# Expert weights in 8 KB rows from mixed buffers, and the second expert's slots mirrored

## The chip, the cores and the metric

The kernel runs on one core of a Trainium2 chip. The metric is the device time in microseconds (us) of one execution. The kernel before took 617.83 us, the median of three runs (617.82 to 617.93).

## The reference

One layer of a streaming encoder on 512 tokens of 1024 channels, in float32: a mixer (pooling and sparse attention), cross-attention to 256 memory tokens, and a mixture of experts (MoE). The change touches how the MoE gets its weights and its rows. Cut to that:

```python
g_sel  = argmax(hf @ wg_router + bg_router)              # one of 4 groups per token
e_in   = (hf @ we_router + be_router)[group g_sel]       # 8 experts of that group
top_v, top_i = top_k(e_in, 2)                            # two experts per token
top_w  = softmax(top_v) * softmax(group logits)[g_sel]
for each expert e of 32:                                 # w_gate, w_up: 1024 x 256; w_down: 256 x 1024
    out += (silu(hf @ w_gate[e]) * (hf @ w_up[e]) * gate[:, e]) @ w_down[e]
```

The weights of the 32 experts are 96 matrices of 1 MB. With these inputs an expert is chosen by 16 to 53 tokens.

## The kernel before

**Tiles and stages.** Tokens lie in 4 blocks of 128 (t = 0 to 3). The mixer and the cross-attention take the first 350 us or so; large products there are made of three products of split operands (`mm3`, L346 to L348). For each block, `wo_proj(t)` then adds the attention output to the residual tile `x[t]`, and `ffn_in(t)` turns `x[t]` by PE transposes (L1115) into `xT`, copied out by ACT (L1117, first half) and DVE (L1123), sums its squares on ACT (L1118), writes `x[t]` to the two DRAM tensors `hd` and `out` on ACT's DMA queue (L1119, L1121), and makes the router's logits on PE (L1129), which DVE scales (L1133) and ranks.

**The MoE.** Experts are taken in 16 pairs. A pair has 128 rows, one per partition: the first expert's tokens in partitions 0 to 63 (`CAP` = 64), the second's in 64 to 127. `select` (L1030) compares each token's place within its expert with a row of numbers 1 to 64 (`iota`), and `tables` makes from that, by matmuls, the token number of each row; empty rows get a number out of range, and are left out by the DMA. `fetch` gathers the rows of a pair from `hd` into one of two `g` buffers, `turn_rows` transposes them, `gate_up` and `down` are the matmuls (L1037), with the SiLU on ACT (L1227), and the result is added into `out` by an indirect DMA on POOL's queue (L1253, one row of 4 KB per token). The `g` buffers are zeroed once by ACT (L1019), in `buffer`, which the program calls after `ffn_in(3)`; the scheduler puts the instructions ahead of that block's copy on ACT.

**Buffers and loads.** Weights, split operands and other tiles live in slots of 4 KB per partition: 42, and 8 more once the attention's own pool is closed. A free list gives the slot that has been free longest. `Stream` keeps the list of loads in order and issues the next one, on SP's queue (L251), whenever enough slots are free (`pump`, called at each `put`). An expert matrix is two loads of 512 KB, one for each half of its rows (c = 0, 1), of 4 KB per partition: 192 loads in the order gate, up, down of a pair, half by half and expert by expert. SP's DMAs and ACT's share 8 completion lanes; a DMA waits for the one before it on its lane.

**The mark.** When the gates are known, SP issues a DMA of four bytes, `mark` (L1290), which stands in program order ahead of all loads that the program issues later: no load listed behind it starts earlier. 38 half matrices are listed ahead of it. Behind it comes the last write to `out` (L1291), then the loads. Ahead of both, in SP's queue, stands the read of `nover` (L1309), the number of extra passes, which is 0 with these inputs.

## Time and profile before

| | us |
|---|---|
| median of three runs | 617.83 |
| the profiled execution | 616.63 |
| its span, first to last instruction | 614.4 |
| PE busy | 554.3 (90%) |
| DVE, ACT, POOL busy | 303.7, 193.9, 114.0 |
| mean granted TensorE clock | 0.98 |

The profile is one execution. PE is the matmul engine, PEld its weight load, DVE, ACT and POOL the vector, scalar and GpSimd engines, SP the queue that issues the loads. In a list in order of time a row is start (us), duration (us), engine, line, operation, output<-input with sizes, and in brackets the idle time of the engine ahead of it and what ended it. A name with a q (SPq, ACTq) is an instruction of the engine's queue, such as the issue of a DMA. In a table by stretch a row has the stretch, its length, then busy time and number of instructions of each engine, the granted clock, the mean busy share of the 16 DMA engines and what they moved in GB/s. Queue q1 holds SP's loads, q10 ACT's writes, q0 the indirect DMAs; a row of a queue has packets, MB and the time of its packets as a share of 16 engines. A share above 1 comes from packets that overlap on an engine.

### The profile page before, as it was taken

To read this page: it belongs to the slowest core of one execution; us is meant where nothing else is said; L and a number is where in the kernel's file an instruction comes from. 1 tells how busy PE (TensorE), PEld (TensorE's weight loads), DVE (VectorE), ACT (ScalarE), POOL (GpSimd) and SP (SyncE) were. 2 spreads that over 40 slices of the span, in tenths; PEclk is the share of its full clock that TensorE was granted. 3 is DMA by queue.
4 is the path that set the end of the run, shared out by engine and by line. 5 is a ranking of instruction groups with operands and counts; after the bars stand their busy time and mean duration, and the time that the engine had idled before them with its cause. 6 is when DMAs were issued, how large, how long until landed. Compare 5 with 4: busy or idle time off the path is not lost. (4 is left out here: it accounts for less than half of the span.)

```text
span 614.4 us, 9117 instructions
## 1 busy us (share of the span) xinstructions
PE 554.3 (90%) x3414; PEld 384.8 (63%) x3414; DVE 303.7 (49%) x767; ACT 193.9 (32%) x368; POOL 114.0 (19%) x92
## 2 busy tenths in 40 slices
PE   8998989999999999999989879999999997778871
PEld 4786766888777777788868755555555543344430
DVE  3398999999976756544434632122223211111200
ACT  4374534434456557764432200000010000000000
POOL 0334330201372000030000111111112210111111
PEclk8998998999999999999999999999999999999896
DMA  8963022226661201128999699999999999999961
GB/s 286 387 214 103 2 69 86 87 66 226 209 237 36 79 1 35 67 73 254 351 328 375 232 375 408 396 379 385 368 381 359 344 356 369 371 361 361 367 219 28
DMA packets 52836, 147.87 MB, mean 241 GB/s; under 512 B 10290, under 2 KB 11058, under 8 KB 52786
## 3 DMA queue, kind: packets, MB, share of 16 engines
q1 hardware_dynamic: 47170, 135.15, 60.1%
q0 software_dynamic: 4608, 8.40, 5.6%
q10 hardware_dynamic: 1008, 3.67, 1.5%
q8 instruction: 29, 0.48, 0.3%
q14 instruction: 21, 0.17, 0.1%
HBM read 142.99 MB, written 12.58 MB: 253 GB/s over the span
## 5 line engine op out<-in xcount | busy, mean ns | idle before, releaser
L1037 PE MATMUL mm<-s,s 128*64 128x256 f32 x1024 | 124.6, 385 | 22.7 <-DMA s<-in_w_up_dram 9.8
L346 PE MATMUL mm<-s,s 128*128 128x512 f32 (+1 forms) x320 | 131.8, 415 | 1.1 <-ACT s L261 0.9
L347 PE MATMUL mm<-s,s 128*128 128x512 f32 (+1 forms) x320 | 127.6, 399 | 0.3 <-DVE s L268 0.3
L348 PE MATMUL mm<-s,s 128*128 128x512 f32 (+1 forms) x320 | 127.6, 399 | 0.0
L1037 PEld LDWEIGHTS mm<-s,s 128*64 128x64 f32 x1024 | 75.1, 137 | 68.3 <-ACT sg L1227 16.7
L1228 DVE SCALAR_TENSOR_TENSOR sg<-mm,gc,sg 128x256 f32<-128x256 f32 x16 | 7.7, 484 | 131.6 <-PE mm L1037 131.6
L346 PEld LDWEIGHTS mm<-s,s 128*128 128x128 f32 (+1 forms) x320 | 60.3, 189 | 18.2 <-issue 3.4
L1037 PE MATMUL mm<-s,hT 128*64 128x512 f32 x256 | 68.2, 604 | 3.4 <-DVE hT L1237 1.6
L348 PEld LDWEIGHTS mm<-s,s 128*128 128x128 f32 (+1 forms) x320 | 60.7, 190 | 13.8 <-issue 0.9
L347 PEld LDWEIGHTS mm<-s,s 128*128 128x128 f32 (+1 forms) x320 | 60.7, 190 | 13.5 <-issue 1.2
L1253 POOL DMA_INDIRECT out_dram<-s,idx x16 | 25.3, 1584 | 194.7 <-DVE s L1086 160.7
L263 POOL TENSOR_TENSOR s<-s,s 128x1024 fp32r<-128x1024 f32 x17 | 41.8, 2467 | 73.5 <-ACT s L261 73.5
L261 ACT CAST s<-s 128x1024 fp32r<-128x1024 f32 (+1 forms) x42 | 42.5, 1021 | 34.5 <-DMA s<-in_xattn_wkv_dram 8.1
L1250 ACT COPY s<-mm 128x512 f32<-128x512 f32 x16 | 9.4, 586 | 130.3 <-PE mm L1037 130.3
L1037 PEld LDWEIGHTS mm<-s,hT 128*64 128x64 f32 x256 | 20.1, 138 | 42.0 <-issue 24.3
L1251 DVE COPY s<-mm 128x512 f32<-128x512 f32 x16 | 11.1, 692 | 59.4 <-PE mm L1037 59.4
L1227 ACT ACTIVATE sg<-mm,gc 128x256 f32<-128x256 f32 x16 | 7.6, 473 | 101.3 <-PE mm L1037 101.3
L263 DVE TENSOR_TENSOR s<-s,s 128x1024 fp32r<-128x1024 f32 (+1 forms) x25 | 28.9, 1159 | 6.2 <-ACT s L261 4.8
L591 DVE MAX8 m<-s 128x8 f32<-128x256 f32 (+2 forms) x48 | 26.6, 553 | 0.3
L592 DVE MATCH_REPLACE8 s<-m,s 128x256 f32<-128x256 f32 (+2 forms) x48 | 26.0, 541 | 0.0
L687 ACT ACTIVATE p<-p,rsm,fq 128x128 f32<-128x128 f32 (+3 forms) x32 | 20.6, 646 | 6.6 <-DVE rsm L685 6.5
L356 PE MATMUL sc<-s,s 64*128 64x256 f32 (+3 forms) x216 | 22.0, 323 | 0.0
(212 smaller groups left out, 682.0 us busy)
## 6 DMA issues: line engine op xcount, KB each, us to landing
s<-in_w_up_dram SPq DMA_DIRECT2D x64, 512.0 KB
s<-in_w_gate_dram SPq DMA_DIRECT2D x64, 512.0 KB
s<-in_w_down_dram SPq DMA_DIRECT2D x64, 512.0 KB
s<-in_w_in_dram SPq DMA_DIRECT2D x20, 512.0 KB
s<-in_x_dram SPq DMA_DIRECT2D x8, 512.0 KB
s<-in_xattn_wkv_dram SPq DMA_DIRECT2D x8, 512.0 KB
s<-in_w_out_dram SPq DMA_DIRECT2D x8, 512.0 KB
s<-in_xattn_wq_dram SPq DMA_DIRECT2D x4, 512.0 KB
```

The costliest lines, as they stand in the source:

```text
L261: act.copy(hi, raw)
L263: eng.tensor_tensor(lo[:, c], raw[:, c], f32(hi[:, c]), op=OP.subtract)
L346: pe.matmul(ps, ah, bh, start=start, stop=False)
L347: pe.matmul(ps, ah, bl, start=False, stop=False)
L348: pe.matmul(ps, al, bh, start=False, stop=stop)
L356: pe.matmul(ps[i], a(i, qa), b(i, qb), start=(n == 0), stop=(n == 2), skip_group_check=True)
L591: dve.max(m8, a)
L592: dve.match_replace(a, m8, a, TAKEN)
L687: act.activation(ph, ph, AF.Exp, bias=m[:, h, 1:2], scale=f[:, h:h + 1], accum_out=m[:, h, 2:3])
L1037: return tc.keep_in_program_order(pe.matmul(*a, **k))
L1251: dve.tensor_copy(y[:, 512:], py[1])
L1253: pool.indirect_dma_start(out=out, out_offset=bass.IndirectOffsetOnAxis(ap=tabs_.pop(i)["idx"], axis=0), in_=y, in_offset=None, bounds_che ...
```

## The change

Three things change. First, the buffers: 18 slots of 4 KB and 12 of 8 KB (4 more of 8 KB later) stand in place of 42 (and 8) of 4 KB. The capacity is the same. A pair of split operands takes one 8 KB slot, and `N_OWN` slots of 4 KB are held back for the MoE's own tiles. Second, an expert matrix is one entry of the stream. It is loaded whole, by one DMA of 1 MB in rows of 8 KB per partition, into an 8 KB slot; where two 4 KB slots have been free for longer, it is loaded as two halves into these. In the MoE that makes 117 loads, 75 of 1 MB and 42 of 512 KB, in place of 192. Third, the second expert of a pair is mirrored: its first token has partition 127, its second 126, and so on, through a second row of numbers 64 to 1 beside `iota` (`seat`). Besides, the read of `nover` is written ahead of the first pass.

```diff
-NSLOT = 42
-NSLOT2 = 8
+N_ONE, N_TWO, N_TWO_MORE, N_OWN = 18, 12, 4, 7
...
+    def get_pair(self, shape, dt):
+
+        if not self.free2:
+            return [self.get(shape, dt) for _ in range(2)]
+        s = self.free2.pop(0)
+        t = self.tile(s, [P, 2, *shape[1:]], dt)
+        self.left[s] = 2
+        return [self.hold(t[:, i], s, t) for i in range(2)]
+
+    def get_whole(self, shape):
+
+        two, ones = self.free2[:1], self.free1[:2] if len(self.free1) >= 2 + self.owed else []
+        when = lambda v: max(self.freed[s] for s in v)
+        half = [shape[0], shape[1] // 2, *shape[2:]]
+        if two and (len(ones) < 2 or when(two) <= when(ones)):
+            s = self.free2.pop(0)
+            t = self.tile(s, shape, F32)
+            self.left[s] = 2
+            h = shape[1] // 2
+            return [(slice(None), t)], [self.hold(t[:, i * h:(i + 1) * h], s, t) for i in range(2)]
+        h = shape[1] // 2
+        parts = [self.get(half, F32) for _ in range(2)]
+        return [(slice(i * h, (i + 1) * h), p) for i, p in enumerate(parts)], parts
+
+    def room(self, shape, keep):
+        if int(np.prod(shape[1:])) <= 1024:
+            return len(self.free) >= 1 + keep
+        return len(self.free) >= 2 + keep and (bool(self.free2) or len(self.free1) >= 2 + self.owed)
 
     def take_out(self):
-        return self.free.pop(0)
+        self.owed = max(0, self.owed - 1)
+        return self.free1.pop(0)
...
     def do_load(src, shape):
+        if int(np.prod(shape[1:])) > 1024:
+            loads, parts = S.get_whole(shape)
+            for c, t in loads:
+                ins = sp.dma_start(t, src[:, c])
+                if held_back:
+                    tc.keep_in_program_order(ins)
+            return parts
...
-        hi, lo = S.get(shape, F32R), S.get(shape, F32R)
+        hi, lo = S.get_pair(shape, F32R)
...
+    seat = keep.tile([P, 2, CAP], F32, name="seat")
+    act.copy(seat[:, 0], iota)
+    dve.tensor_scalar(seat[:, 1], iota, -1.0, float(CAP + 1), op0=OP.mult, op1=OP.add)
...
-        s4 = sels[j].rearrange("p t (e c) -> p t e c", c=CAP)
+        s4 = sels[j].rearrange("p t (i e c) -> p t i e c", e=2, c=CAP)
         for t in tiles:
-            dve.tensor_tensor(s4[:, t], posp[:, t, 4 * j:4 * j + 4, None].to_broadcast([P, 4, CAP]),
-                              iota[:, None, :].to_broadcast([P, 4, CAP]), op=OP.is_equal)
+            dve.tensor_tensor(s4[:, t], posp[:, t, 4 * j:4 * j + 4].rearrange("p (i e) -> p i e", e=2)[:, :, :, None]
+                              .to_broadcast([P, 2, 2, CAP]), seat[:, None].to_broadcast([P, 2, 2, CAP]), op=OP.is_equal)
...
-            for c in range(2) if 0 <= i < NPR else ():
-                for k, e in enumerate(pairs[i]):
-                    w = A[f"w_{name}"][e]
-                    if name == "down":
-                        src, shape = w.rearrange("(p k) d -> p k d", k=2)[:, c], [P, D]
-                    else:
-                        src, shape = w.rearrange("(p k) f -> p k f", k=NC)[:, 4 * c:4 * c + 4], [P, 4, FF]
-                    ST.add((n, i, name, k, c), src, shape, eng="raw")
+            for k, e in enumerate(pairs[i] if 0 <= i < NPR else ()):
+                m = {"down": 2, "gate": NC, "up": NC}[name]
+                ST.add((n, i, name, k), A[f"w_{name}"][e].rearrange("(p k) f -> p k f", k=m), [P, m, 2048 // m], eng="raw")
...
     ST.pump()
+    n_extra = nc.values_load(nover, min_val=0, max_val=T // CAP - 1)
     moe_pass(0)
-    n_extra = nc.values_load(nover, min_val=0, max_val=T // CAP - 1)
```

The orders of the instructions move in three places. First ACT at the last block of tokens, before: `x[2]`'s write to `out`, the zeroing of the two `g` buffers, the copy of `xT` for block 3, its sum of squares and the write to `hd`.

```order
L1121 DMA out_dram<-s_150_1569 128x1024 [waits DMAHW3_49]
L1019 ACTIVATE s_272_3360<-cst 128x1024 [waits PE_49]
L1019 ACTIVATE s_273_3362<-cst 128x1024 [waits PE_49]
L1117 COPY s_270_3302<-tr 128x512 [waits PE_49]
L1118 ACTIVATE s_271_3303,s_2922<-s_151_1583 128x1024 [waits DVE_49]
L1119 DMA hd<-s_151_1583 128x1024 [waits DMAHW7_49]
L1196 ACTIVATE s_274_3385<-s_274_3385 128x4x4 [waits DVE_49]
```

And now, with the same places at L1207, L1105, L1203, L1204, L1205:

```order
L1207 DMA out_dram<-s_111_1530 128x1024 [waits DMAHW4_49]
L1105 ACTIVATE s_199_3275<-cst 128x1024 [waits DMAHW2_49,DMAHW4_49,PE_49,Activation_49]
L1203 COPY s_197_3217<-tr 128x512 [waits PE_49]
L1204 ACTIVATE s_198_3218,s_2867<-s_112_1544 128x1024 [waits DVE_49]
L1205 DMA hd<-s_112_1544 128x1024 [waits DMAHW7_49]
L1105 ACTIVATE s_200_3277<-cst 128x1024 [waits DVE_49,PE_49,Activation_49]
L1283 ACTIVATE s_201_3300<-s_201_3300 128x4x4 [waits DVE_49]
```

The first zeroing now has a slot that held `x[2]`, and waits for lanes 2 and 4, those of `x[2]`'s writes to `hd` and `out`; the copy stands behind it. The second zeroing stands behind the write of block 3.

Then SP from the mark on, before:

```order
L1309 TENSOR_LOAD nover [waits DVE_49]
L1309 ISA x2
L1290 DMA mark<-s_274_3385 1x1 [waits DMAHW0_49,DVE_49]
L1291 DMA out_dram<-s_151_1583 128x1024 [waits DMAHW1_49]
L251 DMA s_275_3418<-in_w_up_dram 128x1024 [waits DMAHW2_49]
L251 DMA s_276_3420<-in_w_up_dram 128x1024 [waits DMAHW3_49,PE_49,Activation_49]
L251 DMA s_277_3422<-in_w_down_dram 128x1024 [waits DMAHW4_49,Activation_49]
L251 DMA s_278_3424<-in_w_down_dram 128x1024 [waits DMAHW7_49,DMAHW5_49,DMAHW1_49]
L251 DMA s_279_3426<-in_w_down_dram 128x1024 [waits DMAHW6_49,PE_49]
L251 DMA s_282_3497<-in_w_down_dram 128x1024 [waits PE_49]
L251 DMA s_283_3499<-in_w_gate_dram 128x1024 [waits DMAHW0_49,PE_49]
```

And now:

```order
L1377 DMA mark<-s_201_3300 1x1 [waits DMAHW1_49,DVE_49]
L1378 DMA out_dram<-s_112_1544 128x1024 [waits DMAHW2_49]
L328 DMA s_202_3333<-in_w_up_dram 128x2048 [waits DMAHW3_49,PE_49]
L328 DMA s_203_3335<-in_w_down_dram 128x1024 [waits DMAHW4_49,Activation_49]
L328 DMA s_204_3336<-in_w_down_dram 128x1024 [waits DMAHW5_49,DMAHW7_49,DMAHW2_49,PE_49]
L1395 TENSOR_LOAD nover [waits DVE_49]
L1395 ISA x2
L328 DMA s_207_3422<-in_w_down_dram 128x2048 [waits DMAHW6_49,PE_49]
L328 DMA s_208_3424<-in_w_gate_dram 128x1024
L328 DMA s_209_3425<-in_w_gate_dram 128x1024 [waits DMAHW0_49]
```

Behind the mark there are now one whole matrix and two halves (4 halves in all) ahead of a whole `down` matrix that waits for PE; the read of `nover` stands behind the mark and not ahead of it.

And SP at the end of the first pass, before (`down` of the last pair, half by half):

```order
L251 DMA s_456_4824<-in_w_down_dram 128x1024 [waits DMAHW0_49,PE_49]
L251 DMA s_457_4826<-in_w_down_dram 128x1024 [waits DMAHW1_49,PE_49]
L251 DMA s_458_4828<-in_w_down_dram 128x1024 [waits DMAHW2_49,PE_49]
L251 DMA s_460_4844<-in_w_down_dram 128x1024 [waits DMAHW3_49,PE_49]
L1310 COMPARE_AND_BRANCH
```

And now, by whole matrices:

```order
L328 DMA s_323_4615<-in_w_up_dram 128x2048 [waits DMAHW5_49,PE_49]
L328 DMA s_324_4635<-in_w_up_dram 128x2048 [waits DMAHW6_49,PE_49]
L328 DMA s_325_4637<-in_w_down_dram 128x2048 [waits DMAHW7_49,PE_49]
L328 DMA s_327_4653<-in_w_down_dram 128x2048 [waits DMAHW0_49,PE_49]
L1397 COMPARE_AND_BRANCH
```

The last DMA of the pass is the second expert's whole `down` matrix; before it was the second half of it.

## Rows read from the trace of the kernel before

**Rows 1.** busy tenths in 40 slices of the span, from the page

```profile
PE   8998989999999999999989879999999997778871
...
DMA  8963022226661201128999699999999999999961
```

**Rows 2.** by stretch: busy of PE, PEld, DVE, ACT, POOL, clock, DMA share, GB/s

```profile
375.00:400.00 25.00, 23.31 (x174) 13.18 (x172) 7.03 (x18) 2.12 (x4) 5.31 (x4) 1.00 1.03 398
```

**Rows 3.** ACT, L1227, start, us; one per pair

```profile
451.51 0.47 ACT L1227 ACTIVATE sg<-mm,gc 128x256 f32<-128x256 f32 x1 [5.33 <-PE mm L1037]
...
465.47 0.47 ACT L1227 ACTIVATE sg<-mm,gc 128x256 f32<-128x256 f32 x1 [6.49 <-PE mm L1037]
...
563.74 0.47 ACT L1227 ACTIVATE sg<-mm,gc 128x256 f32<-128x256 f32 x1 [5.41 <-PE mm L1037]
...
588.33 0.47 ACT L1227 ACTIVATE sg<-mm,gc 128x256 f32<-128x256 f32 x1 [5.99 <-PE mm L1037]
```

**Rows 4.** as 2, from the router to the first pair

```profile
344.00:347.00 3.00, 2.21 (x26) 2.12 (x25) 2.76 (x20) 0.52 (x2) 0.00 (x0) 1.00 0.40 161
347.00:350.00 3.00, 2.16 (x20) 2.00 (x19) 2.01 (x14) 0.00 (x0) 0.54 (x1) 1.00 0.08 29
```

**Rows 5.** SP queue, start, us, from 337 us

```profile
337.66 1.06 SPq L251 DMA_DIRECT2D s<-in_w_up_dram  x2
349.60 0.73 SPq L1290 DMA_DIRECT2D mark<-s  x1
...
350.79 1.21 SPq L251 DMA_DIRECT2D s<-in_w_up_dram  x2
352.10 6.43 SPq L251 DMA_DIRECT2D s<-in_w_down_dram  x4
358.63 2.11 SPq L251 DMA_DIRECT2D s<-in_w_gate_dram  x3
```

**Rows 6.** ACT in order of time, the last token block

```profile
332.76 0.36 ACTq L1121 DMA_DIRECT2D out_dram<-s  x1
...
338.40 1.05 ACT L1019 ACTIVATE s<-cst 128x1024 f32<-128x1024 f32 x1 [1.46 <-PE mm L348]
339.36 0.57 ACT L1117 COPY s<-tr 128x512 f32<-128x512 f32 x1
339.83 1.06 ACT L1118 ACTIVATE s<-s 128x1024 bf16<-128x1024 f32 x1
```

**Rows 7.** DMA packets by queue, 334 to 342 us

```profile
q1 hardware_dynamic: 585, 2.14, 69.2%
q10 hardware_dynamic: 288, 1.05, 32.1%
```

**Rows 8.** PE, the last router projection, L1129

```profile
339.98 1.98 PE L1129 MATMUL mm<-s,s 128*128 128x36 f32 x16
```

**Rows 9.** DVE behind it

```profile
343.38 0.26 DVE L1133 SCALAR_TENSOR_TENSOR s<-mm,s,rgb 128x36 f32<-128x36 f32 x1 [0.66 <-POOL s L244]
```

**Rows 10.** PE, first pair, gate matmuls

```profile
356.24 3.67 PE L1037 MATMUL mm<-s,s 128*64 128x256 f32 x32 [0.33 <-DVE s L1086]
```

**Rows 11.** as 2, full queues: rows of 2 KB, then of 4 KB

```profile
20.00:28.00 8.00, 8.00 (x36) 6.14 (x35) 1.72 (x5) 1.49 (x2) 4.78 (x2) 1.00 1.04 398
585.80:590.00 4.20, 3.08 (x25) 1.95 (x27) 0.00 (x0) 0.47 (x1) 1.55 (x1) 1.00 1.03 415
```

**Rows 12.** as 2, around the last weights

```profile
590.00:592.00 2.00, 1.83 (x16) 1.05 (x14) 0.00 (x0) 0.00 (x0) 0.00 (x0) 1.00 1.01 318
...
594.00:598.60 4.60, 4.08 (x12) 1.06 (x12) 0.42 (x1) 0.00 (x0) 0.00 (x0) 1.00 0.06 20
```

**Rows 13.** as 2, in the last scatter

```profile
607.00:607.50 0.50, 0.00 (x0) 0.00 (x0) 0.00 (x0) 0.00 (x0) 0.00 (x0) 0.50 0.38 74
```

**Rows 14.** PE, a down projection in mid-stage

```profile
375.21 3.60 PE L1037 MATMUL mm<-s,hT 128*64 128x512 f32 x16
```

**Rows 15.** PE, the last one

```profile
598.87 1.93 PE L1037 MATMUL mm<-s,hT 128*64 128x512 f32 x6 [0.15 <-SPq L1310]
```

More of the change, by code (lines that the diff above doesn't have):

```diff
@@ L61, with __init__ @@
 class Slots:
-    def __init__(self, pool, n):
-        self.pools, self.free, self.n, self.where = {}, [], 0, {}
-        self.on_put = lambda: None
-        self.more(pool, n)
-    def more(self, pool, n):
-        self.pools.update({s: pool for s in range(len(self.pools), len(self.pools) + n)})
-        self.free += list(self.pools)[-n:]
-    def get(self, shape, dt):
-        s = self.free.pop(0)
-        self.n += 1
-        t = self.pools[s].tile(shape, dt, tag=f"s{s}", name=f"s{s}_{self.n}")
-        self.where[id(t)] = (s, t)
-        return t
+    def __init__(self, pool, ones, twos):
+        self.pool_of, self.free1, self.free2, self.spare = {}, [], [], []
+        self.where, self.left, self.n, self.clock = {}, {}, 0, 0
+        self.freed = {}
+        self.owed = N_OWN
+        self.on_put = lambda: None
+        self.more(pool, ones, twos)
@@ new lines, in more, with free, tile @@
+    def more(self, pool, ones, twos):
+        for k, (free, n) in enumerate(((self.free1, ones), (self.free2, twos))):
+            for _ in range(n):
+                s = len(self.pool_of)
+                self.pool_of[s] = pool
+                self.freed[s] = 0
+                free.append(s)
+    @property
+    def free(self):
+        return range(len(self.free1) + 2 * len(self.free2) + len(self.spare))
+    def tile(self, s, shape, dt):
+        self.n += 1
+        return self.pool_of[s].tile(shape, dt, tag=f"s{s}", name=f"s{s}_{self.n}")
@@ new lines, in hold @@
+    def hold(self, v, s, of):
+        self.where[id(v)] = (s, of, v)
+        return v
+    def get(self, shape, dt):
+        if self.free1:
+            s = self.free1.pop(0)
+            return self.hold(self.tile(s, shape, dt), s, None)
+        n = int(np.prod(shape[1:]))
+        names = "abc"[:len(shape) - 1]
+        at = next((p for p in self.spare if p[2] == dt), None)
+        if at is None:
+            s = self.free2.pop(0)
+            t = self.tile(s, [P, 2, 1024], dt)
+            self.left[s] = 1
+            half = 0
+            self.spare.append((s, t, dt))
+        else:
+            self.spare.remove(at)
+            s, t, _ = at
+            self.left[s] += 1
+            half = 1
+        v = t[:, half, :n]
+        if len(names) > 1:
+            v = v.rearrange(f"p ({' '.join(names)}) -> p {' '.join(names)}", **dict(zip(names, shape[1:])))
+        return self.hold(v, s, t)
@@ L87, in put @@
+    again = tile
     def put(self, *tiles):
+        self.clock += 1
         for t in tiles:
-            self.free.append(self.where.pop(id(t))[0])
+            s, of, _ = self.where.pop(id(t))
+            if of is None:
+                self.free1.append(s)
+            else:
+                self.left[s] -= 1
+                if self.left[s]:
+                    continue
+                self.spare = [p for p in self.spare if p[0] != s]
+                self.free2.append(s)
+            self.freed[s] = self.clock
@@ L130, in pump @@
                 self.out_next()
-            elif (self.n_load < len(self.items) and len(self.S.free) >= 1 + keep
+            elif (self.n_load < len(self.items) and self.S.room(self.items[self.n_load][2], keep)
                   and (len(self.raw) < self.raw_max)):
@@ L503, in evac_k @@
         if t % 2 == 0:
-            kT[t // 2] = [S.get([P, 2, 4, P], F32R) for _ in range(2)]
+            kT[t // 2] = S.get_pair([P, 2, 4, P], F32R)
         WV.defer(PRM['lat'], lambda: split_T(qr, kT[t // 2][0][:, t % 2], kT[t // 2][1][:, t % 2], ("kT", t)))
@@ L601, in load_bands @@
     def load_bands():
-        pw["b"] = [S.get([P, 1024], F32R) for _ in range(2)]
+        pw["b"] = S.get_pair([P, 1024], F32R)
         pw["w"] = S.get([P, 4, P], F32)
@@ L752, in memory @@
         dve.tensor_tensor(gqk, vecs[:, V_QN:V_QN + 1], vecs[:, V_KN:V_KN + 1], op=OP.mult)
-        kmT.extend(S.get([P, MH, MT], F32R) for _ in range(2))
+        kmT.extend(S.get_pair([P, MH, MT], F32R))
         vm.append(S.get([P, 2, 512], F32))
@@ L831, in transposed @@
     def transposed(t):
-        hl = [S.get([P, NC, P], F32R) for _ in range(2)]
+        hl = S.get_pair([P, NC, P], F32R)
         for k in range(2):
@@ L1217, in gate_up @@
         for u, name in enumerate(("gate", "up")):
-            W = {(k, c): ST.take((n, i, name, k, c)) for c in range(2) for k in range(2)}
+            W, held = expert(n, i, name)
             for c in range(NC):
@@ L1240, in down @@
     def down(n, i, hT):
-        W = {(k, c): ST.take((n, i, "down", k, c)) for c in range(2) for k in range(2)}
+        W, held = expert(n, i, "down")
         y = own("y", i % 2, [P, D], F32)
```

20 lines of the change are left out of this document (11 added, 9 removed).

## The prediction

> **What bounds the kernel now.** I read the slices of the span first, then the table by stretch, then the places where a saturated engine stops. The slices [rows 1] show two regimes: PE full and the DMA engines mostly idle for the first half, then both full from slice 24 on, the MoE. From 375 us the DMA share is 1.03 at 398 GB/s [rows 2]. Which of the two sets the pace there is read from the SiLU of each pair [rows 3]: 13.96 us from 451.51 to 465.47, where PE eats weights fetched ahead, but 24.6 us from 563.74 to 588.33, near the end, where PE waits for weights. So the end of the kernel is the end of the DMA stream that starts behind the mark, plus a tail. In front of it lies a hole: the DMA share is 0.40 in 344 to 347 us and 0.08 in 347 to 350 [rows 4], because SP issues a load at 337.66, then nothing until the mark at 349.60 [rows 5]. A us lost by the mark, or a us in which the queues run dry behind it, is a us at the end. At the far end one engine works alone: 318 GB/s in 590 to 592 us, then 20 GB/s at a share of 0.06, one of sixteen, until the last matmuls start at 598.87 [rows 12, 15].
>
> **The change part by part.** All times are against the profiled execution (616.63 us; span 614.4 and 2.2 us around it). The median shown is 1.20 us above it, and I add that at the end.
>
> *The zeroing on ACT.* This is the part that I think costs most. Before, the second zeroing starts at 338.40 and the copy of block 3 follows at 339.36 [rows 6]; neither waits for a DMA. Now the first zeroing waits for the writes of `x[2]`, and the copy stands behind it. The write to `out` is issued at 332.76 [rows 6]. Between 334 and 342 us ACT's queue moved 288 packets of 1.05 MB in all [rows 7], which is exactly the two writes of 512 KB, so they are through by about 342.0. The zeroing then runs to 343.06 (1.06), the copy to 343.63 (0.57), and the router's matmuls, 1.98 us [rows 8], to 345.6. The other branch, the sum of squares behind the copy (1.06 us) and the power on POOL, ends at about the same time. DVE's scaling of the logits started at 343.38 [rows 9] and would start at 345.7: the gates, the mark and the first gather are 2.3 us later, with the queues already dry. Bounds: 1.0, if the writes land 1.3 us sooner; 4.8, if they land 2.5 us later because each write packet of 4 KB now takes turns with load packets of 8 KB (the queue is then through as late as 344.5, where the share drops in [rows 4]). Value +2.3.
>
> *Loads behind the mark.* Before, nine halves follow the mark between 350.79 and 360.7 (2, 4 and 3 in [rows 5]), each as soon as one slot is free. Now four halves can go, and the fifth entry, a whole `down` matrix, needs both halves of an 8 KB slot, which the first gate matmuls hold: these run from 356.24 for 3.67 us [rows 10], so it is issued at 359.9, and nothing behind it can overtake it. The four halves, the last write and two gathers are 2.1 + 0.5 + 0.45 MB, about 3.05 MB (the gathers are 112 rows of 4 KB by the routing), 7.5 us at 410 GB/s, between [rows 2] and [rows 11], from about 352.5: dry from 360 to the first bytes of the new load. Those come 2 us after its issue by my estimate; the write issued at 332.76 [rows 6] had all its packets behind 334 [rows 7], so it is more than 1.2. That is 2 us. Bounds 0.5 (the writes and gathers stretch over it) and 4.0 (a second such hole about 372 us, where the next whole loads wait for the second pair). Value +2.0.
>
> *The tail.* The last DMA now brings the whole `down` matrix of the second expert, and each of its packets holds both halves of a row, so only 2 of the 16 matmul instructions of `down` can run before it lands, where 10 could. Sixteen take 3.60 us in mid-stage [rows 14], 0.225 each; the last six took 1.93 [rows 15]. Eight more behind the last byte: +1.8, and at least 1.2 if the last packets' landing is spread.
>
> *Rows of 8 KB.* Nothing in the trace has them. Full queues moved 398 GB/s with rows of 2 KB and 415 with 4 KB [rows 11]: 2.513 and 2.410 us per MB, 0.103 less for a doubling. If it is a fixed cost per row, the next doubling saves half as much, 0.052 us per MB. Behind the mark 60 whole loads bring 62.9 MB: 3.2 us. Bounds: 0 (the rows are cut to 4 KB on the way) and 5 (the whole 0.103 carries over, less what two queues already overlap). Value -3.0. Twice the bytes in flight on the same lanes bring nothing, since the share is 1.03 already [rows 2].
>
> *The mirror.* Does it level the engines? The gather and the scatter give each engine the rows of fixed partitions, and the routing of these inputs (worked out from the reference) fills the low places of each half. In the last scatter, 53 and 34 rows, the share is still 0.38 at 607.0 to 607.5 [rows 13], about five or six of sixteen. If the 16 engines each took four neighbours of 64 partitions, and both experts so, eight engines would have a second helping; if eight engines serve the first half and eight the second, five have it. The row speaks for the second. Then engine sums over all pairs are 86 rows at most in the first half and 101 in the second, and mirroring turns the second eight around: the heaviest is still 101. Value 0; the price if it does level them is the second rival's. The extra row of numbers is one instruction each on ACT and DVE at the very start, where PE does not yet work at its full share [rows 1] and loads set the pace, and the read of `nover` moves off SP's path to the mark, but the gates that the mark waits for come after it on DVE anyway: 0, and half a us either way for the early loads, which I take as covered by PE's full slices [rows 1].
>
> Sum: 2.3 + 2.0 + 1.8 - 3.0 = +3.1 on 616.63, 619.7; with 1.20 for the median, **620.9 us**. All lows together give -2.3, all highs +10.6; they are unlikely together, so the likeliest case's own range is 618.9 to 624.5.
>
> **The rivals.**
>
> *The mirror levels the engines (0.12).* For it: one engine ends seven or eight us behind the others (they stop within 590 to 592, PE's last weights come just before 598.87 [rows 12, 15]), so there is a load to level. Against it: [rows 13]. If the heavy places of the two experts do share engines, the lone stretch goes, up to 8 us, and 620.9 falls to about 613.
>
> *Rows of 8 KB pay and the holes don't show (0.20).* If the writes land early and the 8 KB saving is at its bound, the sum of lows holds: 615.5. For it: the loads are most of the bytes. Against it: both waits stand in the order of the instructions.
>
> *The parts cancel (0.18).* With 8 KB at -4 and the two holes at their lower halves, the sum is between -1.2 and +1.2: 616.6 to 619.
>
> *The mirrored heavy engine is slow (0.05).* The last places of the second half now fill first, so the engine of partitions 92 to 95 and 124 to 127 carries 101 rows and sets the end over 246 us. If it were 1% slower than the one that sets it now, the end would move by 2.5 us: 623.4. It decides as soon as that engine is slower at all, since no other has as much to do. Nothing in the rows shows a slow engine: with all of them full the sum is 415 GB/s [rows 11] and the lone one at the end moves 20 [rows 12], of which its share is near a sixteenth of that. The Trainium skill, on the page "DMA: Bandwidth & Descriptors", section "Latency and other measured facts", says that engines 7 and 15 are usually slower than the rest where POOL issues DMAs; by that rule the result would be on this side, and the trace so far does not bear it out.
>
> *8 KB rows are cut to 4 KB (inside the forecast's 0.45).* Then the third term is 0 and the time 623.9.
>
> **How the numbers follow.** The forecast with its upper end has 0.45, the slow engine 0.05: slower 0.50. Same, 0.18. Faster, 0.32 (0.20 and 0.12). Two tenths of a per cent, 1.2 us, is about what this kernel's measurement can tell. The range reaches down to the second rival, 613, and up to 625, a little above the cut rows with a late write; about 2 in 10 lie outside.
>
> **What would show it.** In the changed profile the first zeroing (L1105) should start about 342 with a DMA as its releaser, and the mark near 352; if the mark is at 349.6, the first term is wrong. SP should issue one `down` load when the first gate matmuls end, with a DMA share under 0.8 in the 3 us around it. The q1 packets should be 8 KB, and full stretches should show 420 to 425 GB/s; 415 would mean no saving. A single engine should still end alone for about 8 us; if all engines end together, the mirror works and I am wrong by its price. Behind the last load 14 matmul instructions should follow.

## The result and the profile after

The changed kernel took 628.52 us (median of 4 runs, 624.53 to 631.62) beside 617.88 us: a ratio of 1.0154, with an interval from 1.0115 to 1.0192. It is slower by 10.6 us, as forecast in sign, but more than three times as much, and above the range that ended at 625. The ratios leave out runs more than 1.5% above the fastest of the same kernel (three of ten in e10, one of six in e6, one of the kernel before in the set with e13 to e15); the medians hold all runs. The profiled execution took 631.62 us, 15.0 more than that of before, so the two traces have 4.4 us more to explain than the medians.

The page after, the same two rows as [rows 1] and between them the granted clock of PE:

```profile
PE   8998998999998899999979788999999997878781
...
PEclk8999999999998899999989669999999999898897
DMA  8954013513744100116899557999999999999931
```

The clock falls to 0.8 in slices 13 and 14 and to 0.6 in slices 23 and 24, where DMA is at half too. Placed on the time axis, by three points that both traces have:

| us | before | after | difference |
|---|---|---|---|
| SP issues the mark | 349.60 | 365.19 | +15.6 |
| mark to the end of the last weights' packets | 248.9 | 246.3 | -2.6 |
| from there to the end of the span | 15.9 | 18.0 | +2.1 |

So the whole loss lies ahead of the mark. The stage that the change is about is shorter. The mark moves by some us from one execution to the next: it is at 350.0, 354.0 and 354.3 in e7, e9 and e15, which are the kernel before up to there, and at 364.5 and 361.9 in e5 and e4, which are the changed one. With these the means are 352.0 and 363.9: the loss ahead of the mark is nearer 12 us than 15.6, and 12 less 3.6 in the stretch plus 2.4 behind it is the 10.6 of the medians.

**Where the 15.6 us come from.** I matched the same DVE instruction in both traces and took the difference of their starts (the lag). It is -0.4 us at 184 us of the kernel before, +8.2 at 210, +9.8 at 315, +14.9 at 344 and +16.0 at 349. The lag of PE's matmuls is -0.4 at 190, +6.9 from 205 to 260 and +9.8 at 315. Two jumps, then: one of 7 us in the softmax of the sparse attention, to which 3 more come up to 315 us, together 10 us that the prediction had at nothing, and one of 6 at the zeroing.

The first jump. In the changed trace ACT, in order of time (start, duration, then in brackets idle time and what ended it):

```profile
180.80 1.05 ACT L343 CAST s<-s 128x1024 fp32r<-128x1024 f32 x1 [2.84 <-DMA s<-in_w_out_dram]
...
182.33 1.99 ACT L343 CAST s<-s 128x1024 fp32r<-128x1024 f32 x2
188.16 1.05 ACT L343 CAST s<-s 128x1024 fp32r<-128x1024 f32 x1 [3.84 <-DMA s<-in_w_out_dram]
189.12 0.49 ACT L769 ACTIVATE p<-p,rsm,fq 128x128 f32<-128x128 f32 x1
...
196.98 1.04 ACT L343 CAST s<-s 128x1024 fp32r<-128x1024 f32 x1 [3.94 <-DMA s<-in_w_out_dram]
```

L343 casts a part of `w_out`; the last four of its eight parts are first used in a sum (L937) that starts at 222.3 us. L769 is the exponential of the softmax, which PE needs now. ACT sits 3.84 us on a load, and the softmax behind it, then 3.94 on the next. In the kernel before the same places read:

```profile
179.79 1.99 ACT L261 CAST s<-s 128x1024 fp32r<-128x1024 f32 x2
186.35 0.50 ACT L687 ACTIVATE p<-p,rsm,fq 128x128 f32<-128x128 f32 x1 [4.57 <-DVE rsm L685]
...
190.19 1.03 ACT L261 CAST s<-s 128x1024 fp32r<-128x1024 f32 x1
```

There the exponential starts at 186.35, and the last cast finds its load there. The orders of the instructions thus move in more than the three places listed with the change: SP's `w_out` loads start 6.4 us later, and one stands behind two loads of `xattn_wq`. Before:

```profile
159.19 19.33 SPq L251 DMA_DIRECT2D s<-in_w_out_dram  x8
```

After, with what SP waited for most from 165 to 195 us (total, times, longest); in the kernel before that is PE, 27.6 us from 158 to 195:

```profile
165.55 19.39 SPq L333 DMA_DIRECT2D s<-in_w_out_dram  x7
186.93 5.16 SPq L333 DMA_DIRECT2D s<-in_xattn_wq_dram  x2
192.13 0.46 SPq L333 DMA_DIRECT2D s<-in_w_out_dram  x1
...
SPq L333 <- POOL s L345: 17.3, 6, 3.8
```

L345 is the subtraction that gives the low part of a split operand. So a load of `w_out` waits until POOL has split an earlier part and its slot is free, and ACT waits for the load. PE's share of the loss, and its clock, in the table by stretch (columns as in [rows 2]), before and after:

```profile
175.00:215.00 40.00, 38.40 (x241) 30.70 (x242) 27.92 (x85) 24.11 (x58) 13.54 (x10) 1.00 0.31 102
```

```profile
175.00:215.00 40.00, 35.24 (x190) 27.80 (x189) 25.41 (x78) 20.84 (x50) 12.14 (x5) 0.91 0.36 116
```

PE works 3.2 us less, and the granted clock is 0.91 in place of 1.00, about another 3 us of the 35 in which it works. PE waits twice for the scaled softmax in that stretch, 1.5 and 2.9 us; before, once, 0.9.

The second jump, ACT again, beside [rows 6]:

```profile
341.50 0.34 ACTq L1207 DMA_DIRECT2D out_dram<-s  x1
352.30 1.06 ACT L1105 ACTIVATE s<-cst 128x1024 f32<-128x1024 f32 x1 [10.23 <-DMA out_dram<-s]
...
353.26 0.57 ACT L1203 COPY s<-tr 128x512 f32<-128x512 f32 x1
353.73 1.06 ACT L1204 ACTIVATE s<-s 128x1024 bf16<-128x1024 f32 x1
```

The write is issued at 341.50, and the zeroing starts at 352.30 with that write as its releaser: 10.8 us, where I had put 9.2. PE then stands for 4.05 us, and its last router projection takes 3.63 us beside the 1.98 of [rows 8]:

```profile
353.88 3.63 PE L1215 MATMUL mm<-s,s 128*128 128x36 f32 x16 [4.05 <-ACT s L1203]
```

The next table shows what follows, beside [rows 4]:

```profile
340.00:350.00 10.00, 9.19 (x58) 7.24 (x56) 5.61 (x25) 1.69 (x3) 0.54 (x1) 1.00 1.00 383
350.00:360.00 10.00, 6.12 (x28) 6.06 (x29) 3.36 (x20) 3.85 (x6) 0.55 (x1) 0.56 0.46 188
360.00:370.00 10.00, 8.27 (x54) 8.10 (x53) 3.89 (x25) 0.31 (x1) 2.29 (x2) 0.67 0.31 96
370.00:380.00 10.00, 9.65 (x64) 8.19 (x64) 2.95 (x8) 1.28 (x1) 0.00 (x0) 0.74 0.57 213
```

PE's clock is 0.56, 0.67 and 0.74 in three stretches of 10 us; within them it is at its lower level, 0.50 or 1.2 GHz, from 353 to 360 and from 366 to 373. The seats' tables, which PE makes from there to the first pair, run at that clock for much of the time. The first SiLU, at 380.27 against 359.98, is 20.3 us late, 4.7 more than the mark. And SP, beside [rows 5]:

```profile
345.88 0.33 SPq L328 DMA_DIRECT2D s<-in_w_up_dram  x1
365.19 0.72 SPq L1377 DMA_DIRECT2D mark<-s  x1
365.97 0.35 SPq L1378 DMA_DIRECT2D out_dram<-s  x1
366.42 0.38 SPq L328 DMA_DIRECT2D s<-in_w_up_dram  x1
366.89 13.65 SPq L328 DMA_DIRECT2D s<-in_w_down_dram  x3
380.60 4.22 SPq L328 DMA_DIRECT2D s<-in_w_gate_dram  x3
```

Behind the mark one whole matrix and two halves go out; the third of the three `down` loads ends at 380.5, when the first gate matmuls have ended. DMA is at 96 GB/s and 213 in the meantime. Yet the stream ends 2.6 us sooner after the mark, since full stretches are faster than those in [rows 11]; the fastest in this trace:

```profile
588.00:598.00 10.00, 6.32 (x24) 2.53 (x24) 2.10 (x4) 0.59 (x1) 0.61 (x1) 0.83 1.01 426
```

### The profile page after: what moved, and what is told of

Read it like the earlier page. It is cut to its first block, busy times and chain, and to the rows that moved or that the text cites. A ratio compares the mean times of both kernels' runs of the same rounds, so it can differ in the third digit from the quotient of the medians.

```text
span 629.5 us, 8959 instructions
## 1 busy us (share of the span) xinstructions
PE 561.3 (89%) x3414; PEld 393.2 (62%) x3414; DVE 309.3 (49%) x768; ACT 194.2 (31%) x369; POOL 116.5 (19%) x92
## 5 line engine op out<-in xcount | busy, mean ns | idle before, releaser
L1123 PE MATMUL mm<-s,s 128*64 128x256 f32 x1024 | 123.0, 386 | 14.6 <-ACT sg L1314 9.5
L1123 PEld LDWEIGHTS mm<-s,s 128*64 128x64 f32 x1024 | 72.7, 138 | 61.5 <-ACT sg L1314 16.8
L1123 PE MATMUL mm<-s,hT 128*64 128x512 f32 x256 | 65.3, 619 | 10.8 <-DMA s<-in_w_down_dram 9.2
L345 POOL TENSOR_TENSOR s<-s,s 128x1024 fp32r<-128x1024 f32 x17 | 42.2, 2492 | 87.7 <-ACT s L343 53.1
L343 ACT CAST s<-s 128x1024 fp32r<-128x1024 f32 (+1 forms) x42 | 42.3, 1021 | 48.1 <-DMA s<-in_w_out_dram 15.8
L345 DVE TENSOR_TENSOR s<-s,s 128x1024 fp32r<-128x1024 f32 (+1 forms) x25 | 31.0, 1242 | 4.8 <-ACT s L343 4.8
L1157 POOL DMA_INDIRECT s<-hd,idx x16 | 17.1, 1067 | 31.5 <-DVE gc L1148 18.1
L769 ACT ACTIVATE p<-p,rsm,fq 128x128 f32<-128x128 f32 (+3 forms) x32 | 20.6, 646 | 4.9 <-DVE rsm L767 4.8
## 6 DMA issues: line engine op xcount, KB each, us to landing
s<-in_w_gate_dram SPq DMA_DIRECT2D x14, 512.0 KB, 15.6
```

Source lines behind the costliest of these rows:

```text
L343: act.copy(hi, raw)
L345: eng.tensor_tensor(lo[:, c], raw[:, c], f32(hi[:, c]), op=OP.subtract)
L769: act.activation(ph, ph, AF.Exp, bias=m[:, h, 1:2], scale=f[:, h:h + 1], accum_out=m[:, h, 2:3])
L1123: return tc.keep_in_program_order(pe.matmul(*a, **k))
L1157: pool.indirect_dma_start(out=buffer("g", i % NG_BUF, [P, D]), out_offset=None, in_=hd, in_offset=bass.IndirectOffsetOnAxis(ap=tabs_[i]["i ...
```

## The experiments

Every run was compared with the kernel before on the same chip, so the ratios count; the median of the kernel before itself differs by up to 2.2 us from one set of runs to the next. "Mark" and "to last weights" are from the run's own trace, one for each, and among kernels that are the same up to there the mark differs by up to 4.7 us; e10's trace is of an execution 4 us above its median and is left out.

The theory, by the traces above: two waits of ACT, and no slower stream, make the loss. One is for loads of `w_out`, which come late since a request takes the head of its own list of slots and not the slot free for longest; the other is for the writes of `x[2]`, whose tile is put back, and so reused by the zeroing, too early. The rivals: the early loss comes from another engine or from the number of 4 KB slots; the second jump is the first one carried on; the stream itself is slower, by the rows or by the mirror.

| run | median us | ratio (interval) | mark | mark to last weights |
|---|---|---|---|---|
| changed kernel | 628.52 | 1.0154 (1.0115 to 1.0192) | 365.2 | 246.3 |
| e5 the same again | 628.95 | 1.0133 (1.0093 to 1.0173) | 364.5 | 244.4 |
| e1 late return of x[2] | 621.80 | 1.0026 (0.9994 to 1.0059) | 356.8 | 243.6 |
| e2 longest-free slot | 620.36 | 1.0016 (0.9988 to 1.0044) | 356.7 | 244.1 |
| e3 both | 620.66 | 1.0020 (0.9984 to 1.0056) | 354.9 | 244.3 |
| e12 both, w_out on DVE | 616.74 | 0.9947 (0.9911 to 0.9982) | 352.3 | 244.7 |
| e13 e1, w_out on DVE | 622.36 | 1.0085 (1.0052 to 1.0117) | 358.1 | 242.4 |
| e8 30 + 6 slots, late return | 632.66 | 1.0211 (1.0175 to 1.0247) | 363.5 | 245.2 |
| e6 halves of 4 KB | 628.66 | 1.0107 (1.0066 to 1.0148) | 360.7 | 252.2 |
| e4 no mirror | 624.56 | 1.0091 (1.0054 to 1.0129) | 361.9 | 244.8 |
| e9 before, mirror alone | 620.98 | 1.0015 (0.9979 to 1.0052) | 354.0 | 248.7 |
| e7 before, dealt | 603.96 | 0.9751 (0.9709 to 0.9794) | 350.0 | 234.5 |
| e15 the same again | 605.02 | 0.9777 (0.9727 to 0.9826) | 354.3 | 234.8 |
| e10 changed, dealt | 615.10 | 0.9904 (0.9868 to 0.9939) | | |
| e11 e3, dealt | 612.46 | 0.9881 (0.9838 to 0.9924) | 355.4 | 236.8 |
| e14 e12, dealt | 604.07 | 0.9807 (0.9769 to 0.9844) | 349.6 | 232.4 |

### The wait for the writes of x[2]: e1

```diff
-        if t < 3:
+        if t < 2:
             S.put(x.pop(t))
...
     for i in range(2):
         fetch(i)
+    S.put(x.pop(2))
```

> The changed kernel, but the slot of x[2] is given back only after the g buffers are zeroed and the first two gathers are written, so neither zeroing nor the copy of block 3 waits for the writes of x[2]. Theory A (the wait on ACT costs 5 us by itself and 4 to 5 more, because PE idles 10 us and then runs the tables at the low clock): 628.5 falls to 618 to 621, the zeroing or copy of block 3 starts under 1 us behind PE's transposes, granted clock in the 25 us around the mark near 1.0. Rival B (the writes and loads are slow because 1 MB loads fill the queues; the wait is a symptom): the mark moves by under 2 us and the time stays at 626 or more.

Theory A, though not to its full size: the ratio falls to 1.0026, from 1.0154 and 1.0133, which is 6.6 to 7.9 us; 621.80 us is just above the 618 to 621 expected. Beside e4, which lacks only the mirror and ran on the same chip, it is 2.8 us. The mark moves from 365 to 356.8, and the clock is at 0.84 and 0.99, where it was 0.56 and 0.67:

```profile
350.00:360.00 10.00, 8.25 (x65) 8.07 (x65) 6.38 (x40) 2.42 (x4) 2.27 (x2) 0.84 0.29 92
360.00:370.00 10.00, 9.06 (x80) 7.05 (x81) 2.95 (x8) 1.76 (x2) 0.00 (x0) 0.99 0.96 345
```

The lag goes from 8.4 at 315 to 7.4 at 349, in place of 9.8 to 16.0. What is left is the first jump. (PE idled 4.05 us in the changed kernel, not the 10 of the expectation: 10.23 was ACT's wait.)

### The early loss: e2, e3, e8, e12, e13

```diff
     def get(self, shape, dt):
-        if self.free1:
+        two = [p[0] for p in self.spare if p[2] == dt] + self.free2[:1]
+        if self.free1 and not (two and self.freed[two[0]] < self.freed[self.free1[0]]):
```

> The changed kernel, but a 4 KB request takes whichever has been free longer, a 4 KB slot or half of an 8 KB one. Theory A (w_out's loads wait for the few 4 KB slots still in use, and ACT's casts of them stand ahead of the softmax): lag of 7 us at 210 us goes to under 2, time about 619 to 622. Rival B (w_out is late for another reason, such as lanes or order of the list): lag at 210 us stays at 5 to 7, time 626 to 630.

Between the two. The lag at 315 falls from 9.8 to about 4, and the total by 8 us; the exponential starts at 185.8. But the lag at 210 is still 4.8: at that place theory A as put is refuted. Nor are all of these 8 us the early loss: in e2 the copy of block 3 also stands ahead of the zeroing, and from 335 to 349 us the lag grows by 2.5 in place of 6.2. The loads of `w_out` do come sooner, the same in e2 and e3; in e3:

```profile
160.02 16.18 SPq L334 DMA_DIRECT2D s<-in_w_out_dram  x8
```

> Both edits together. Theory A: the two losses are separate, so 608 to 613, below the kernel before, since the MoE stage itself is 5 us shorter (235.7 against 240.9 us from the first SiLU to the last copy). Rival B: 624 or more.

A miss: 620.66 in place of 608 to 613. The two edits are not additive, since in e2 the copy of block 3 already stood ahead of the zeroing (at 343.80, the zeroing at 347.54). e3's trace shows what now holds the softmax, though no load does, DVE first, then POOL:

```profile
189.70 5.89 DVE L777 TENSOR_SCALAR p<-p,rsm 128x128 f32<-128x128 f32 x8
```

```profile
190.44 4.64 POOL L346 TENSOR_TENSOR s<-s,s 128x1024 fp32r<-128x1024 f32 x2 [2.38 <-ACT s L344]
```

The eight scalings do not all get slower: one by one, six take 0.28 to 0.30 us, and the two that start while POOL subtracts the low part of `w_out` take 2.38 and 2.52, until just after the subtraction ends. The changed kernel, where POOL had nothing then, has eight in 1.66; the kernel before has one such, of 2.41:

```profile
193.32 1.66 DVE L776 TENSOR_SCALAR p<-p,rsm 128x128 f32<-128x128 f32 x8
```

```profile
190.56 3.79 DVE L694 TENSOR_SCALAR p<-p,rsm 128x128 f32<-128x128 f32 x8
```

Ahead of that ACT's cast, and with it the exponential, waited 2.71 us for POOL (184.54 us).

To test that, the splits of `w_out` went from POOL to DVE (e12, on top of e3):

```diff
-           eng="dddp ppdd dddp dpdd dpdd dddd dppp dpdp ppdp dppp")
+           eng="dddp ppdd dddp dpdd dpdd dddd dppp dddd dddd dppp")
```

> The run with the longest-free slot and the late return of x[2], with the splits of w_out taken from POOL and given to DVE. There DVE's four softmax scalings took 5.10 us beside a POOL subtraction that began at the same time, 1.66 us for eight in the changed kernel where none ran. Theory C (POOL's and DVE's instructions hold each other up, and that keeps the lag of 4 to 5 us at 210): the scalings take under 2 us, the lag at 210 falls under 3 and the total is 616 to 619 against 620.7. Rival (DVE then has 1.24 us more work per matrix in the way): same or slower, 620 to 624.

Theory C holds: 616.74, the eight scalings take 1.66 us again, the lag at 210 is 2.6 at most, and the clock stays at 1.00 in the stretch in which the changed kernel had 0.91:

```profile
175.00:215.00 40.00, 36.58 (x230) 28.66 (x229) 31.11 (x89) 23.98 (x54) 1.37 (x5) 1.00 0.32 110
```

> The changed kernel with the late return of x[2]'s slot and w_out's splits on DVE, but without the longest-free slot. If the early loss (8 to 10 us at 315) is the choice of slot, which makes w_out's loads late, ACT's casts still stand ahead of the softmax: lag at 315 6 to 9, total 619 to 623 against 621.8. If it is POOL's splits alone: lag at 315 under 4, total 615 to 618, as with all three edits (616.7).

Without the choice of the longest-free slot the same edit gives nothing (622.36, ratio 1.0085, beside 621.80 and 1.0026 of e1): the lag at 315 is 7.6. The stretch of the softmax says it plainly, e3 first, then e13:

```profile
175.00:215.00 40.00, 34.98 (x202) 27.75 (x201) 26.68 (x76) 21.04 (x50) 13.19 (x10) 0.91 0.32 108
```

```profile
175.00:215.00 40.00, 34.70 (x204) 27.59 (x203) 28.80 (x84) 21.87 (x51) 0.69 (x4) 0.91 0.41 123
```

With one edit alone PE has as little and as slow work there as in the changed kernel; with both it has more, at 1.00. From 186 to 210 us PE's lag grows by 7.3 us in the changed kernel, 7.1 in e3, 6.3 in e13 and 2.7 in e12. So the first cause is the choice of the slot, which makes `w_out` late; POOL's collision takes its place once the loads are in time, and only both edits together free the softmax. The smaller growth up to 315, in the cross-attention, goes with the choice of the slot: 2.9 us in the changed kernel, 3.7 in e13, none in e3 and e12.

```diff
-N_ONE, N_TWO, N_TWO_MORE, N_OWN = 18, 12, 4, 7
+N_ONE, N_TWO, N_TWO_MORE, N_OWN = 30, 6, 4, 7
```

> The changed kernel with 30 slots of 4 KB and 6 of 8 KB (the same capacity) and the slot of x[2] given back late: 46 whole matrices and 100 halves. Theory A (too few 4 KB slots delay w_out's loads): the lag at 210 us falls under 3 us and the total is 614 to 618, below the kernel with only the late slot (621.8). Rival B (the order of the early work, not the number of slots): lag at 210 us 5 to 7, total 620 to 624.

It went the other way: 632.66, and the lag at 315 is 14.7. ACT waits 5.0 us for `xattn_wkv` at 137 to 142 us and 3.5 for `xattn_wq` in the stretch of the softmax; that the 8 KB slots for pairs run short instead is the likely reason, but was not tested. So more 4 KB slots do not help. What e2, e3 and e12 speak for is that a request took the head of one of two lists even where the other had had a slot free for longer.

### Rows of 8 KB: e5, e6

```diff
             loads, parts = S.get_whole(shape)
+            if len(loads) == 1:
+                t, h = loads[0][1], shape[1] // 2
+                loads = [(slice(i * h, (i + 1) * h), t[:, i * h:(i + 1) * h]) for i in range(2)]
             for c, t in loads:
```

> The changed kernel, with every whole matrix brought into its 8 KB buffer by two DMAs of 512 KB in rows of 4 KB. If rows of 8 KB are what shortens the MoE stage (first SiLU to last copy 235.7 us, 240.9 before): the stage gets longer by 3 to 6 us, full stretches show 415 to 420 GB/s in place of 430, but the writes of x[2] land in 5 to 8 us in place of 10.7, so the total moves by less, -3 to +4. If the stage is shorter for another reason (more in flight, weights fetched farther ahead): the stage stays within 1.5 us and the total falls by the gain at the writes.

> The changed kernel as it is, beside the other runs of this call. Both theories: 624 to 632, ratio to the kernel before 1.010 to 1.019. It is the measure for the mirror: without it the ratio was 1.0091 (1.0054 to 1.0129). If mirroring does nothing, the two ratios overlap; if it loads a slow engine, this one is higher by 0.005 or more.

From the mark to the last weights 252.2 us with halves, 244.4 in the control measured beside it and 246.3 in the first trace of the changed kernel: the rows of 8 KB, with fewer DMAs for the same bytes, are worth 6 to 8 us there, by one trace of e6. And 252.2 against 248.9 is what the holes behind the mark cost, 3.3. The bytes agree: 20 us behind the mark 76.5 MB of loads are still to come in e6 and 75.2 before, and e6 keeps 1.0 to 1.6 MB more to come up to 190 us behind it. The median hardly moves, as expected, since the mark comes 3.8 us sooner (in the traces e6 is still 2.1 us slower). Of the 3.8 us, 2.1 are there at 335 us already; the rest is the first zeroing, which starts 7.9 us behind the issue of the write in e6, beside packets of 4 KB, and 9.7 in e5.

### The mirror and the engines: e4, e9, e7, e10, e15

e4 leaves the second row of numbers unmirrored; e9 adds the mirror to the kernel before (e4's edit first, then the lines that e9 adds; its `select` compares with `seat` as the changed one does):

```diff
-    dve.tensor_scalar(seat[:, 1], iota, -1.0, float(CAP + 1), op0=OP.mult, op1=OP.add)
+    dve.tensor_scalar(seat[:, 1], iota, 1.0, 0.0, op0=OP.mult, op1=OP.add)
```

```diff
+    seat = keep.tile([P, 2, CAP], F32, name="seat")
+    act.copy(seat[:, 0], iota)
+    dve.tensor_scalar(seat[:, 1], iota, -1.0, float(CAP + 1), op0=OP.mult, op1=OP.add)
```

> The changed kernel with the second expert's slots not mirrored. If mirroring only turns the load of the second eight engines around: no difference, 625 to 631. If it loads a slow engine: 2 to 4 us faster than 628.5. If it levels engines: 5 or more us slower.

> The kernel before with the mirrored slots alone. If mirroring only turns the load of the second eight DMA engines around: ratio within 0.004 of 1, mark to last weights 248 to 250 us (248.9 before), one engine still alone for 6 to 8 us at the end. If it loads a slow engine: 2 to 5 us slower. If it levels engines: 5 us or more faster.

Nothing either way: 1.0015, with an interval that holds 1, and 248.7 us from the mark to the last weights beside 248.9. One engine is still alone at the end, as in [rows 12]:

```profile
592.00:596.00 4.00, 3.27 (x26) 1.67 (x24) 0.00 (x0) 0.47 (x1) 1.17 (x1) 1.00 1.01 376
596.00:598.00 2.00, 1.48 (x12) 0.70 (x8) 0.41 (x1) 0.00 (x0) 0.00 (x0) 1.00 0.43 86
598.00:602.60 4.60, 3.54 (x12) 1.06 (x12) 0.50 (x2) 0.00 (x0) 0.00 (x0) 1.00 0.06 21
```

e4's median is 4 us below the control's, which by its own expectation would speak for a slow engine. But its stretch behind the mark is 244.8 against 244.4, and the intervals overlap; the difference lies ahead of the mark, where the mirror does nothing. Nor is the engine that now has the most rows slower: the packets of 4 KB of the one engine left at the end take 159 ns in a load and 327 in the scatter, in e9 as in the kernel before.

Then the mapping that [rows 13] speak for was used: eight neighbours in rank go to eight engines, on the kernel before (e7).

```diff
+    seat = keep.tile([P, CAP], F32, name="seat")
+    act.copy(seat.rearrange("p (a b c) -> p a b c", a=2, b=8), iota.rearrange("p (a c b) -> p a b c", a=2, c=4))
...
-                              iota[:, None, :].to_broadcast([P, 4, CAP]), op=OP.is_equal)
+                              seat[:, None, :].to_broadcast([P, 4, CAP]), op=OP.is_equal)
```

> The kernel before, with the places of both experts dealt over the engines: the row of numbers is permuted so that the first eight tokens of an expert fall on eight engines, the next eight again. Theory A (the DMA engine with 101 rows sets the end; each row costs it about 0.16 us in the gather and 0.33 in the scatter): the heaviest engine falls to about 70 rows, 15 us less work for it; the lone engine's stretch at the end goes, and the time falls by 8 to 15 us, to 604 to 611. Rival B (the lone engine is slow for another reason, or PE would set the end anyway): less than 3 us.

15.8 us faster. The stretch from the mark to the last weights falls by 14.4 us, to 234.5, near the 15 us of work that the heaviest engine was to lose. The engines still do not end together: the share is 0.26 in the last 4.5 us, four engines' worth.

```profile
575.00:580.00 5.00, 4.27 (x33) 2.45 (x32) 0.00 (x0) 0.47 (x1) 0.56 (x1) 1.00 0.90 308
580.00:584.50 4.50, 3.33 (x13) 1.11 (x12) 0.91 (x2) 0.00 (x0) 0.00 (x0) 1.00 0.26 91
```

On the changed kernel (e10) both rows of numbers are dealt, and the second expert is no longer mirrored:

```diff
-    act.copy(seat[:, 0], iota)
-    dve.tensor_scalar(seat[:, 1], iota, -1.0, float(CAP + 1), op0=OP.mult, op1=OP.add)
+    deal = iota.rearrange("p (a c b) -> p a b c", a=2, c=4)
+    act.copy(seat[:, 0].rearrange("p (a b c) -> p a b c", a=2, b=8), deal)
+    dve.tensor_copy(seat[:, 1].rearrange("p (a b c) -> p a b c", a=2, b=8), deal)
```

> The changed kernel with dealt places (the first eight tokens of an expert on eight engines) in place of the mirror. Theory: the DMA engines' load and the rest of the change are separate, so the stretch from mark to last weights falls from 244 to 246 to about 230 and the total from 628.7 to 612 to 617, ratio 0.985 to 0.998. Rival: with rows of 8 KB the late mark and the holes behind it bind instead of the engine, and less than 6 us is gained.

615.10, a ratio of 0.9904 beside 1.0133 to 1.0154 of the changed kernel: 2.3 to 2.5%, some 14 to 15 us, about what the same edit gives on the kernel before.

e15 repeats e7 beside e14, on the same chip, for the comparison below.

> The kernel before with dealt places once more, for the same chip and hour as the run with all edits: 602 to 606, ratio 0.971 to 0.979.

### All causes together: e11, e14

e11 is e3 with the edit of e10, and e14 is e12 with it.

> The changed kernel with the longest-free slot, the late return of the slot of x[2], and dealt places. Theory: 620.7 less 14 is 606, and rows of 8 KB give some more now that PE's own pace (13.4 us a pair) is nearer: 600 to 607, beside 604 for the kernel before with dealt places. Rival (PE becomes the bound, rows of 8 KB give nothing then): 608 to 612.

> All edits: longest-free slot, late return of x[2]'s slot, w_out's splits on DVE, dealt places. If the parts add up: 616.7 less 10 to 14, 603 to 607, mark near 352 and mark to last weights 234 to 237. If rows of 8 KB and the lighter engine add up beside PE's pace, up to 599.

e11 misses its range by 5 us, and its rival's by half a us: the early loss is still in it (mark at 355.4). e14 has neither loss (mark at 349.6, as before) and beats both kernels: 604.07, ratio 0.9807. Beside it the kernel before with dealt places has 605.02, ratio 0.9777: the same within the intervals. e14's stream is 2.4 us shorter than e15's, and its end from the last weights on 3 us longer (18.7 against 15.7 us). So once the engines are level, the longer end takes back what the stream still gains from the change.

## Why the prediction was wrong, point by point

**The step that failed** is the one put last: "0, and half a us either way for the early loads, which I take as covered by PE's full slices". It cost some 10 us in the trace. A full slice shows that PE does not wait now; it says nothing of what stands in ACT's queue between PE and its next operand. ACT had slack in total (175 us busy in the first 350), but a cast that waited for a load stood in its queue ahead of the exponential, and the next such cast ahead of the copies that PE needs. That one `w_out` load now comes behind two of `xattn_wq` stands in the order of SP's instructions; that the others are late, and what is queued behind their casts, the prediction did not ask. Shown by e3, e12 and e13 together, all with the late return of `x[2]`: with the longest-free slot and `w_out` away from POOL the mark is at 352.3 and the ratio 0.9947, against 354.9 and 1.0020 with the first edit alone and 358.1 and 1.0085 with the second alone. Against e1, which has neither, the two edits are worth 4.9 us by the ratios. The 2.7 us that are left at e12's mark, in one profile each, stay open; e7, e9 and e15, whose early part is the kernel before's, have their marks between 350.0 and 354.3.

**The zeroing on ACT** was the right mechanism with the right place, and mis-sized: +2.3 forecast, about 5 by the ranking and 6 with the mark (e1: 6.6 to 7.9 us by the ratios). The copy of block 3 is 4.1 us late beyond the early lag, where the sum had 3.7: the write took 10.8 us from issue to release, not 9.2, but was issued 1.1 sooner. What the sum did not have at all is PE's clock, which fell after the stall: the router's last projection takes 3.63 us in place of 1.98. The upper bound of 4.8 was too low for the same reason.

**Loads behind the mark**: +2.0 forecast, 3.3 by e6, inside the bounds of 0.5 to 4.0. In the changed kernel's own trace it is more: 20 us behind the mark 77.4 MB are to come, 2.2 more than before, which at 400 GB/s is 5.5 us; the first pair is later there, at the low clock.

**The tail**: +1.8 forecast, +2.1 by the traces, but the agreement is in part luck, since the reason is another. All 16 matmuls now follow in one piece, beside [rows 15], and they wait for `hT`, not for the last `down` load, whose packets ended at 611.48. What is late is the whole `up` load of the same expert:

```profile
606.97 3.67 PE L1123 MATMUL mm<-s,s 128*64 128x256 f32 x30 [0.40 <-DMA s<-in_w_up_dram]
...
612.23 3.65 PE L1123 MATMUL mm<-s,hT 128*64 128x512 f32 x16 [0.52 <-DVE hT L1324]
```

The forecast's picture, 2 matmuls, a wait for SP's load and then 14, is what e6 shows, where the halves are loaded one by one:

```profile
609.80 1.07 PE L1126 MATMUL mm<-s,hT 128*64 128x512 f32 x2 [0.52 <-DVE hT L1327]
612.04 3.65 PE L1126 MATMUL mm<-s,hT 128*64 128x512 f32 x14 [1.17 <-SPq L1400]
```

**Rows of 8 KB**: -3.0 forecast, -7.8 by e6 against e5 (-5.9 against the first trace), beyond the bound of -5. The rows are not cut: the packets have 8 KB. The extrapolation was for packets alone, and its 398 GB/s is of a stretch in which half the bytes came in rows of 4 KB. The packets' own times are the better source: 84, 159 and 309 ns (medians) for 2, 4 and 8 KB, which is 75 ns for each 2 KB and 9 for each packet. So a row of 8 KB saves 9 ns, and 60 whole loads, 480 rows on each of 16 engines, 4.3 us. The rest I can't split between fewer DMAs and the deeper queue: that wasn't tried.

**The mirror**: 0 forecast, 0 found (e9, and e4 beside e5). The rival that it levels the engines is refuted. The one of a slow engine is not borne out: its 2.5 us do not show in the stretch behind the mark, nor in the packets' times. (That the lone engine's 20 GB/s is near a sixteenth of 415 was misread, since that is 26; rows of the scatter, 327 ns each, make the difference.) For that one the Trainium skill ("DMA: Bandwidth & Descriptors", "Latency and other measured facts") says that engines 7 and 15 are usually the slower ones; with the largest load of rows turned to the other end of the second eight engines, the stretch behind the mark is 248.7 beside 248.9 us, so this case does not bear it out. The same page's section "The descriptor swizzle" gives partitions 0 to 63 to eight engines and 64 to 127 to the other eight, in groups of four; e7, which was dealt by that rule, and the 14.4 us that it brought agree with it.

**The sum of the rival in which the parts cancel** does not come out as put: with -4 for the rows, the tail at +1.8 and the two holes between their lower bounds and their values it is -0.7 to +2.1, not -1.2 to +1.2. Nothing measured hangs on it.

## What to carry to other kernels

When a change moves loads, follow each of them to the engine that first touches it, and list what stands behind that instruction in its queue: the use that counts is the first touch, not the matmul. When the wait is gone, look again at the same place, since another one may take over, as POOL's did in e3. A PE stall has a second price in the granted clock: here a copy that was 4.1 us late made the mark 5.8 us late. And before rows are moved to level the DMA engines, find from a lone scatter which partitions share an engine: mirroring kept the heaviest load whole, dealing by eights took 15 us off the kernel.

## What the runs showed of the hardware

- A DVE scaling of 128 x 128 elements that takes 0.28 us took 2.38 and 2.52 where it started beside a POOL subtraction of two 128 x 1024 tensors, and ended with it (e3; 2.41 in the kernel before).
- Full stretches of loads moved 426 GB/s with rows of 8 KB, 415 with 4 KB and 398 with half the bytes in rows of 2 KB. The packets took 309, 159 and 84 ns for 8, 4 and 2 KB, which is 9 ns each beside 75 for each 2 KB.
- Around a PE stall of 4.05 us the granted clock fell from 1.00, and it was 0.56, 0.67 and 0.74 in the three stretches of 10 us from 350 us on, in which PE was busy for 6.1, 8.3 and 9.7.
- The second of two writes of 512 KB beside loads had its last packet 8.3 to 10.4 us behind its issue in the traces with rows of 8 KB (changed kernel, e1, e2, e4, e5) and 7.4 to 9.1 in those with rows of 4 KB (kernel before, e6, e7, e9, e15). The ranges overlap, so that larger rows hold up a write is not shown.
